# Attention scores on one core: the first key load as two halves of 128 partitions, or as four loads of every fourth partition

## The chip, the cores and the metric

The kernel runs on one NeuronCore of a Trainium2 chip. The metric is device time in microseconds (us) for one execution. The engines are TensorE (PE, with its weight loads shown as PEld), VectorE (DVE), ScalarE (ACT), GpSimd (POOL) and SyncE (SP). Loads and stores run on the core's 16 DMA engines. SyncE and ScalarE issue them here, each in a queue of its own.

## The reference

```python
def setup_inputs():
    batch, heads, seq, dim = 8, 8, 512, 64
    return {"q": randn(batch, heads, seq, dim), "k": randn(batch, heads, seq, dim)}   # float32

def reference(q, k):
    scale = 1.0 / np.sqrt(q.shape[-1])
    return (np.einsum('bhqd,bhkd->bhqk', q, k) * scale).astype(np.float32)
```

For each of 64 pairs of batch and head, a 512 x 64 matrix q is multiplied with the transpose of a 512 x 64 matrix k. The inputs have 8.4 MB each, the output has 67.1 MB.

## The kernel before, in words

**Units and loads.** The batches are taken two at a time: four units (`UNITS`), each with 2 MB of k and 2 MB of q. A load (`load`, L68) brings one of these into one half of a buffer `big` in the on-chip memory: 128 partitions with one row of 16 KB each. The partition number is made of the index (s h m), which runs over half of the heads and over blocks of 64 sequence rows, and of (b x), which is the batch of the unit and the half of the heads. (b x) has four values and is the fast part: partition = 4 x (s h m) + (b x). In DRAM the 32 rows of one value of (b x) lie one behind the other, 512 KB in all, and the four values lie 512 KB apart.

**The first k load** is cut in two halves of the rows (L74 to L78): each half goes to all 128 partitions with 8 KB a row. SyncE issues the first half, ScalarE the second, both ahead of the program's opening barrier (L80). Each half has its own semaphore (`halves`).

**SyncE's order** is written out by hand. After the barrier it issues the next five loads (L91: q of unit 0, then k and q of units 1 and 2). It then waits twice for casts, because unit 3 shares a buffer with unit 1, and issues k and q of unit 3 (L93 to L95). Then come sixteen stores of 4 MB (L96 to L99), each behind a wait for the results of its group, and at last a wait for all stores (L102).

**GpSimd** (L105 to L122) turns each load into bf16 and writes it in another order into `xb`: two casts for each load, one for each half of the rows. For the first k load the first cast waits for the first half alone and the second cast for the second half. Each load that has been cast counts up `ready`.

**VectorE** transposes blocks of 32 x 32 out of `xb` into `kT` (L148, keys) and `qz` (L156, queries), and shares with ScalarE the work of taking results out of PSUM: ScalarE multiplies by the scale at L186 (80 tiles), VectorE at L189 (48 tiles). **TensorE** does 256 matmuls (L140).

**Buffers.** Three buffers `big` of 4 MB serve the loads and then the stores in turn (`store_buffer`, L62). TensorE does not start a group before the store that used its buffer three groups earlier has landed, nor, for the first groups, before the loads in that buffer have been cast.

Of the kernel before, what the change touches and what calls it, by code (L numbers as in the profile page):

```python
# [5 lines left out]
def kernel(  # L6
# [5 lines left out]
    nc = tc.nc  # L12
    B, H, S, D = q.shape
    scale = 1.0 / (D ** 0.5)
    P = 128
# [4 lines left out]
    R = S // M  # L20
# [12 lines left out]
    names = ["ready", "zeroed", "pe", "act", "dve"]  # L33
    sem = {name: nc.alloc_semaphore(name) for name in names}
    load_sems = [nc.alloc_semaphore(f"load{n}") for n in range(2 * UNITS)]
    halves = [load_sems[0], nc.alloc_semaphore("load0b")]
    store_sems = [nc.alloc_semaphore(f"store{n}") for n in range(3)]


# [18 lines left out]
    def xf(v):  # L58
        return bigs[(0, 1, 2, 1)[v]].rearrange("p x i k -> p (x i k)").rearrange(
            "p (x s c) -> p x s c", x=2, s=2)  # L60
# [4 lines left out]
    def rows(v, x):  # L65
        return (k_r, q_r)[x][v]

    def load(v, x):  # L68
        nc.sync.dma_start(out=xf(v)[:, x].rearrange("p s c -> p (s c)"), in_=rows(v, x)
                          ).then_inc(load_sems[2 * v + x], 16)  # L70

    for s, queue in enumerate((nc.sync, nc.scalar)):  # L74
        first_load = queue.dma_start(
            out=xf(0)[:, 0, s], in_=rows(0, 0)[..., s * R * D // 2:(s + 1) * R * D // 2]
        ).then_inc(halves[s], 16)
        tc.no_tile_sem_insts.add(first_load.ins.name)  # L78
    tc.close()
    tc.compile()  # L80

# [6 lines left out]
        return who, g * takers.count(who) + takers[:p + 1].count(who)  # L88


    for n in range(1, 2 * (UNITS - 1)):  # L91
        load(n // 2, n % 2)
    for x in range(2):  # L93
# [10 lines left out]

    for v in range(UNITS):  # L105
        for x in range(2):
            if v or x:
                nc.gpsimd.wait_ge(load_sems[2 * v + x], 16)
            for s in range(2):
                if v == x == 0:  # L110
                    nc.gpsimd.wait_ge(halves[s], 16)
                src = xf(v)[:, x, s]
                dst = xb[:, 2 * v + x]
                if x == 0:
                    src = src.rearrange("p (w e d) -> p w e d", e=2, d=D)
                    dst = dst[:, s * J // 2:(s + 1) * J // 2].rearrange("p w d e -> p w e d")
                else:
                    src = src.rearrange("p (jj e i d) -> p jj e i d", e=2, i=RO, d=D)
                    dst = dst.rearrange("p (i jj) d e -> p jj e i d", i=RO)[
                        :, s * JJ // 2:(s + 1) * JJ // 2]  # L120
                cast = nc.gpsimd.tensor_copy(out=dst, in_=src)  # L121
            cast.then_inc(sem["ready"], 1)  # L122
# [3 lines left out]
    for pair in range(ALL * PAIRS):  # L126
        g, p = divmod(pair, PAIRS)
        n, i = g % 4 * 2 + p // 4, p % 4 * 2
# [51 lines left out]
    for pair in range(ALL * PAIRS):  # L180
        g, p = divmod(pair, PAIRS)
# [43 lines left out]
```

## Time and profile before

| What | us |
|---|---|
| Median of 6 runs (201.37 to 201.61) | 201.49 |
| The profiled execution | 201.37 |
| Its span, from the first to the last instruction | 200.1 |
| PE busy | 85.4 |
| DVE busy | 154.9 |
| ACT busy | 79.4 |
| POOL busy | 38.9 |
| First half of k, from issue to landing (SyncE) | 5.9 |
| Second half of k, from issue to landing (ScalarE) | 10.5 |
| Stores, from issue to landing, median (longest) | 15.1 (22.8) |

The span begins at the first instruction; all times in views of the profile count from there. A line of the profile's page or of the timeline names the engine, the line of the kernel (L121 is line 121), the operation, what is written and what is read (`xb<-big`) and the shapes. "SPq" and "ACTq" are the issues of transfers by SyncE and ScalarE. An issue is not the transfer: the bytes move afterwards, and the landing is when the last of them is in place. The waits of an engine are listed as: engine and line, what it waited for, microseconds in total, how often, longest.

### The profile page before, as it was taken

How to read it: one execution, taken by the hardware profiler on the slowest of the kernel's cores; microseconds unless marked ns; L12 is line 12 of the kernel's file. 1: busy time of each engine (PE TensorE's matmuls, PEld its weight loads, DVE VectorE, ACT ScalarE, POOL GpSimd, SP SyncE). 2: the span in 40 equal slices, each digit the busy share in tenths (PEclk: the TensorE clock that was granted, in tenths of full speed). 3: DMA queues.
4: the chain of work that ended last, by engine and by line, in shares of the span. 5: the costliest groups of instructions: out<-in, count | busy, mean ns of one | idle time of the engine just before them, and what ended most of it. 6: DMA issues, size and time to landing. Idle time of an engine off the chain costs nothing.

```text
span 200.1 us, 784 instructions
## 1 busy us (share of the span) xinstructions
PE 85.4 (43%) x251; PEld 27.3 (14%) x256; DVE 154.9 (77%) x97; ACT 79.4 (40%) x81; POOL 38.9 (19%) x20
## 2 busy tenths in 40 slices
PE   0000064474932474547355825572374557910000
PEld 0000021121311121112111211121121112200000
DVE  2428959996999899989998999999989996830000
ACT  2000026272763285248423942583347344940000
POOL 0479999986000000000000000000000000000000
PEclk9999999666698597558755896879759555995555
DMA  5999999999999999999999999999999999999996
GB/s 187 442 419 449 426 423 432 419 367 439 439 432 419 432 436 442 414 426 432 449 419 424 436 442 426 419 429 446 436 419 429 436 436 423 423 432 449 426 419 288
DMA packets 5652, 83.94 MB, mean 420 GB/s; under 512 B 400, under 2 KB 400, under 8 KB 400
## 3 DMA queue, kind: packets, MB, share of 16 engines
q1 hardware_dynamic: 5504, 82.84, 97.5%
q10 hardware_dynamic: 144, 1.05, 1.2%
q8 instruction: 2, 0.03, 0.1%
q14 instruction: 2, 0.02, 0.0%
HBM read 16.78 MB, written 67.11 MB: 419 GB/s over the span
## 4 chain that ended last, share of the span: by engine, by line
DVE 54%; DMA 13%; POOL 11%; PE 6%; ACT 4%; issue 1%
DVE qz L156 24%; DVE big L189 18%; DVE kT L148 12%; POOL xb L121 11%; DMA big<-in_q_dram 8%; PE ps L140 6%; DMA big<-in_k_dram 5%; ACT big L186 4%
## 5 line engine op out<-in xcount | busy, mean ns | idle before, releaser
L140 PE MATMUL ps<-kT,qz 128*128 128x512 bf16 x251 | 85.4, 495 | 90.7 <-DVE big L189 57.2
L186 ACT ACTIVATE big<-ps 128x1024 f32<-128x1024 f32 x80 | 78.1, 1028 | 95.2 <-PE ps L140 92.5
L189 DVE TENSOR_SCALAR big<-ps 128x1024 f32<-128x1024 f32 x48 | 57.7, 1218 | 9.7 <-PE ps L140 9.4
L156 DVE STREAM_TRANSPOSE qz<-xb 32x1024 f32<-32x1024 f32 x32 | 64.1, 2003 | 1.2 <-POOL xb L121 0.7
L140 PEld LDWEIGHTS ps<-kT,qz 128*128 128x128 bf16 x256 | 27.3, 119 | 148.3 <-DVE big L189 76.0
L121 POOL CAST xb<-big 128x2048 bf16<-128x2048 f32 x16 | 38.7, 2474 | 9.1 <-DMA big<-in_k_dram 8.4
L148 DVE STREAM_TRANSPOSE kT<-xb 64x1024 f32<-64x1024 f32 x16 | 31.2, 1947 | 7.3 <-POOL xb L121 6.9
L171 DVE MEMSET qz<- 128x4096 uint32 x1 | 3.5, 3472 | 3.5 <-PEq L80 3.5
L186 ACT ACT_TABLE_LOAD x1 | 1.3, 1283 | 2.6 <-PEq L80 2.6
L209 POOL MEMSET const-float32-0.0<- 128x1 f32 x1 | 0.1, 98 | 0.2 <-issue 0.2
L209 POOL MEMSET const-bfloat16-1.0<- 128x1 bf16 x1 | 0.1, 101 | 0.0
L209 POOL MEMSET const-uint8-127<- 128x1 uint8 x1 | 0.1, 101 | 0.0
L209 POOL MEMSET const-float32-1.0<- 128x1 f32 x1 | 0.1, 98 | 0.0
## 6 DMA issues: line engine op xcount, KB each, us to landing
out_dram<-big SPq DMA_DIRECT2D x16, 4096.0 KB, 15.1
big<-in_q_dram SPq DMA_DIRECT2D x4, 2048.0 KB, 17.3
big<-in_k_dram SPq DMA_DIRECT2D x3, 2048.0 KB, 15.1
big<-in_k_dram SPq DMA_DIRECT2D x1, 1024.0 KB, 5.9
big<-in_k_dram ACTq DMA_DIRECT2D x1, 1024.0 KB, 10.5
```

The lines of the kernel that those rows point to most:

```text
L121: cast = nc.gpsimd.tensor_copy(out=dst, in_=src)
L140: ins = pe.matmul(out=pss[pair % 4][:, w, :], lhsT=qz[:, n, i + w], rhs=kT[:, n], start=True, stop=True)
L148: return nc.vector.transpose(out=kw[2 * y * Q:2 * (y + 1) * Q, b % 2 * G:(b % 2 + 1) * G].rearrange("d g (m w) -> d w m g", w=J), in_=xw[s ...
L156: return nc.vector.transpose(out=qw[d:d + Q, b % 2 * G:(b % 2 + 1) * G, :, h * Q:(h + 1) * Q].rearrange("d g i (m jj) -> d i jj m g", jj=J ...
L171: nc.vector.memset(qz, 0.0).then_inc(sem["zeroed"], 1)
L186: nc.scalar.mul(out=o, in_=ps, mul=scale).then_inc(sem["act"], 1)
L189: nc.vector.tensor_scalar(out=o, in0=ps, scalar1=scale, scalar2=None, op0=mult).then_inc(sem["dve"], 1)
L209: nc = _bacc.Bacc("TRN2", target_bir_lowering=False, num_devices=1)
```

## The change

The first k load becomes four loads instead of two. Load n takes one value n of (b x): 512 KB that lie in one run in DRAM, to the 32 partitions n, n + 4, n + 8 and so on, with a full row of 16 KB each. SyncE issues load 0 and ScalarE load 1 ahead of the barrier. SyncE issues loads 2 and 3 after the barrier, ahead of the five loads that stood there. Each load has its own semaphore, and GpSimd waits for all four before its first cast; the two casts themselves stay as they were.

```diff
-    halves = [load_sems[0], nc.alloc_semaphore("load0b")]
+    parts = [load_sems[0]] + [nc.alloc_semaphore(f"load0_{n}") for n in range(1, 4)]
...
-    for s, queue in enumerate((nc.sync, nc.scalar)):
-        first_load = queue.dma_start(
-            out=xf(0)[:, 0, s], in_=rows(0, 0)[..., s * R * D // 2:(s + 1) * R * D // 2]
-        ).then_inc(halves[s], 16)
-        tc.no_tile_sem_insts.add(first_load.ins.name)
+
+    def load_part(queue, n):
+        dst = xf(0)[:, 0].rearrange("p s c -> p (s c)")[n:P:4]
+        return queue.dma_start(out=dst, in_=rows(0, 0)[:, n]).then_inc(parts[n], 16)
+
+    for n, queue in enumerate((nc.sync, nc.scalar)):
+        tc.no_tile_sem_insts.add(load_part(queue, n).ins.name)
     tc.close()
     tc.compile()
...
+    for n in (2, 3):
+        load_part(nc.sync, n)
     for n in range(1, 2 * (UNITS - 1)):
         load(n // 2, n % 2)
...
     for v in range(UNITS):
         for x in range(2):
-            if v or x:
-                nc.gpsimd.wait_ge(load_sems[2 * v + x], 16)
+            for part in [load_sems[2 * v + x]] if v or x else parts:
+                nc.gpsimd.wait_ge(part, 16)
             for s in range(2):
-                if v == x == 0:
-                    nc.gpsimd.wait_ge(halves[s], 16)
                 src = xf(v)[:, x, s]
                 dst = xb[:, 2 * v + x]
```

## The prediction

> **What bounds the kernel now.** I read the profile in this order: the page's busy rows and DMA row, the busy time by stage, SyncE's own waits, the timeline of the first microseconds, the chain of waits, and last the trace's packet and landing records, of which the page prints only the sums.
>
> The page first. The digits are tenths of each of 40 slices; the queue line gives packets, MB and the share of 16 DMA engines' time.
>
> ```profile
> span 200.1 us, 784 instructions
> ...
> DMA  5999999999999999999999999999999999999996
> ...
> q1 hardware_dynamic: 5504, 82.84, 97.5%
> ...
> HBM read 16.78 MB, written 67.11 MB: 419 GB/s over the span
> ```
>
> VectorE, the busiest compute engine, has 77%; the DMA engines have 9 in every slice but the first and the last. The busy time by stage says the same (columns: window, length, busy time and count of PE, PEld, DVE, ACT, POOL, PE clock, DMA share, GB/s):
>
> ```profile
> 0.00:2.10 2.10, 0.00 (x0) 0.00 (x0) 0.00 (x0) 0.00 (x0) 0.20 (x4) 1.00 0.00 0
> 2.10:5.00 2.90, 0.00 (x0) 0.00 (x0) 1.46 (x1) 1.28 (x1) 0.00 (x0) 1.00 1.01 322
> 5.00:13.50 8.50, 0.00 (x0) 0.00 (x0) 2.01 (x1) 0.00 (x0) 4.62 (x2) 1.00 1.03 438
> ...
> 40.00:42.20 2.20, 2.20 (x6) 0.71 (x5) 2.15 (x3) 1.88 (x2) 2.20 (x2) 0.50 1.13 343
> 42.20:177.30 135.10, 75.58 (x225) 24.02 (x228) 125.99 (x82) 70.42 (x73) 5.46 (x3) 0.74 1.01 430
> 177.30:198.20 20.90, 0.00 (x0) 0.00 (x0) 0.00 (x0) 0.00 (x0) 0.00 (x0) 0.56 1.00 427
> ```
>
> For the last 21 us no engine computes at all while the DMA still moves 427 GB/s. SyncE's waits agree:
>
> ```profile
> SPq L98 <- DVE big L189: 141.3, 16, 11.3
> SPq L102 <- DMA out_dram<-big: 22.4, 2, 19.3
> ```
>
> It waits 22.4 us for stores to land after it has issued the last one at 177.3. So when the last result is ready, over two stores of 4 MB are still queued, and compute could be some 10 us later at no cost. The page's chain of waits gives VectorE 54%, but it runs through work that the queue covers: the end is set by how many bytes the DMA engines have to move and by when they are held up.
>
> This can be added up. By the packet records each engine moves 312 rows of 16 KB (median 0.611 us) and 16 rows of 8 KB (0.309 us): 190.6 + 4.9 = 195.6 us. Add 2.15 us before the first byte, some 0.35 us of slow first rows, 0.5 us lost at 40 to 42 us (343 GB/s where 430 is usual), and some 1.3 us by which instruction fetches at 80 to 108 and 159 us put one engine behind: 199.9. The last landing is at 200.0. Nothing that shortens compute is in this sum.
>
> **The change part by part.** *What the compute engines gain is hidden.* Timeline (start, duration, what):
>
> ```profile
> 0.73 0.63 SPq L75 DMA_DIRECT2D big<-in_k_dram  x1
> 0.74 0.66 ACTq L75 DMA_DIRECT2D big<-in_k_dram  x1
> 2.61 0.54 SPq L69 DMA_DIRECT2D big<-in_q_dram  x1
> ...
> 6.72 2.45 POOL L121 CAST xb<-big 128x2048 bf16<-128x2048 f32 x1 [6.28 <-DMA big<-in_k_dram]
> 11.33 31.47 POOL L121 CAST xb<-big 128x2048 bf16<-128x2048 f32 x13 [2.16 <-DMA big<-in_k_dram]
> 13.89 3.97 DVE L148 STREAM_TRANSPOSE kT<-xb 64x1024 f32<-64x1024 f32 x2 [6.87 <-POOL xb L121]
> ```
>
> Today the second half of k lands at 11.28 because ScalarE's rows take turns with the first q load. After the change all four parts stand ahead of q, so at the usual pace k would be complete near 2.15 + 0.35 + 8 x 0.611 + 0.1 = 7.5 us. But POOL now waits for all four before its first cast: casts at 7.5 and 10.0, end 12.4, and VectorE starts 1.4 us earlier than at 13.89. That lead dies at once: q lands at 13.42 today (issue 2.61, 10.8 us to landing) and the bytes ahead of it stay the same, so POOL, which starts q's casts at 13.8, gains at most 0.4 us there. After that a load of 2 MB lands every 4.89 us and POOL's two casts take 4.84, so POOL follows the landings. I cost this part at nothing. What hides it is the queue of stores; without that cover it would be worth at most 0.4 us. The two further waits on POOL hold back only casts of the same k; VectorE's first transpose is behind them, covered as above.
>
> *SyncE's queue.* Two issues more stand at 2.6 and 3.2 us, each 0.53 to 0.63 us by the load rows, so the five loads behind them leave SyncE 1.2 to 1.3 us later: the first q load at 3.85 instead of 2.61. By the first load, bytes start 1.42 us after the issue starts (0.73 to 2.15). So part 3 would start by 4.0 us, part 4 by 4.7, q by 5.3. Parts 1 and 2 give each engine four 16-KB rows, which keep it busy to 2.15 + 0.35 + 4 x 0.611 = 4.95. The margin is 0.9 us; q has more. Cost nothing; without the margin see the rivals. No later load or store moves past another.
>
> *The rows.* Per engine 16 rows of 0.309 us go and 8 rows of 0.611 come: -0.06 us. Two more loads mean two more completion writes on each engine, 9 ns each: +0.02.
>
> *The issue itself.* The stores' issues take 0.372 us, the loads' 0.53 to 0.66. If a load with one plain run of DRAM is issued like a store, the first byte comes 0.26 us earlier. Bounds -0.26 to 0; I take 0, the load rows being nearest.
>
> *How fast the 32-partition loads run.* This is the open cost, and everything hangs on it. Every load and store of this trace covers 128 partitions, eight rows on each engine for a load, and ran at 0.611 us a row with no row of two engines in each other's way. None covers 32 partitions, four apart; how two rows per engine are dealt, and whether engines then get in each other's way, no row shows. Low end: 0.611 us a row, cost 0. High end: engines slow each other to half the pace, 8 x 0.611 = +4.9 us. Between them stands the only place where all engines ran slow, where the last load meets the first store:
>
> ```profile
> 41.00:42.00 1.00, 1.00 (x4) 0.34 (x3) 0.97 (x2) 1.00 (x2) 1.00 (x1) 0.50 0.79 229
> ```
>
> There 39 rows took 0.65 to 1.18 us, mean 0.91. I take that mean for the eight rows: 8 x (0.91 - 0.61) = +2.4 us. I choose the middle row and not the low end because the new loads change exactly what kept the rows even: the one pattern of 128 partitions in which all 16 engines keep step.
>
> [...]
>
> The sum: -0.06 + 0.02 + 0 + 2.4 = +2.4 us. Since the DMA engines have no idle time later, what is lost at the start is still lost at the end. The profiled execution took 201.37 us (its span 200.1 and 1.3 around it), 0.12 below the median of 201.49: 203.8 on it, 203.9 on the median.
>
> **The rivals.**
>
> *The parts run at full pace and nothing else counts.* For it: the same bytes, rows of 16 KB as in every other load, and a gain in compute that is hidden. Against it: only that no such load is in the trace. Sum -0.04: 201.4, within 0.2% (0.4 us, about what a measurement of this kernel can tell from no change).
>
> *A shorter start: faster.* The place is 0.7 to 3.5 us. The issue may shorten by 0.26 us; and four engines took 1.27 to 1.38 us over their first row where the others took 0.97, and stay 0.45 us behind. If reading one plain run evens that out, up to 0.26 + 0.45 + 0.04 = 0.75 us goes, less if another engine is last. It decides once rows run at 0.611 us and more than 0.4 us of the start goes: 200.7 to 201.1, say 200.9. Against it: the first row of any engine has to wait for its first bytes.
>
> *The DMA runs dry* between parts 2 and 3. For it: only 1 MB is queued before SyncE passes the barrier at 2.6 us, where 2 MB was. The first q load's first row came 4.0 us after its issue; if that were its own delay and not the queue ahead of it, part 3 would come at 6.6, 1.67 us after the engines ran out: 203.1. Against it: every engine took its first ScalarE row after exactly seven SyncE rows, the slow engines 0.4 us later than the rest; so that wait counts rows ahead, not time.
>
> *The chain of waits is right* and POOL's earlier start reaches the end: 0.4 us at q, 1.4 at most, so 200.1 to 201.1. Against it: the 22.4 us of queued stores.
>
> **How the numbers follow.** Slowed rows 0.50 (its own range 201.7 to 206.3, from almost none of the cost to all of it; 0.04 of the chance lies under 201.9); full pace 0.26; shorter start 0.14; dry 0.05, nearly all of it slower; chain 0.05. Faster by over 0.2%: 0.14 + 0.04 of the chain = 0.18. Slower: 0.46 + 0.04 = 0.50. Within: 0.26 + 0.04 + 0.02 = 0.32. The likeliest case gives 203.9. The range for 8 in 10 leaves out about 0.1 at the top, the slowed rows nearest to half pace, and 0.1 at the bottom: 200.9 to 205.8.
>
> **What would show it.** Right: k's rows longer than 0.611 us between 2.2 and 10 us; some 300 GB/s from 2 to 12 us, where 403 stands today; q's landing near 15.8 instead of 13.4; every later landing as much later; the rate after 42 us unchanged. Full pace: k complete near 7.5, q still at 13.4. Dry: a gap in the DMA row near 5 us. Shorter start: first byte before 2.1 us, and the whole series of landings earlier by as much. The prediction is wrong above all if eight rows of k take 0.611 us each; then only the start is left to move the end.

## The result, and the profile after

The changed kernel took 201.92 us (median of 20 runs, 201.29 to 202.77) against 201.54 us (median of 40 runs, 201.34 to 201.79) in the same sessions: ratio 1.0022, 95% interval 1.0014 to 1.0029. So it is slower by 0.4 us, where 2.4 us was forecast. Its runs are spread over 1.5 us, those of the kernel before over 0.45. The profiled execution took 202.13 us, with a span of 200.8, 0.76 longer than the span before; it stands in the upper half of the runs, and the profiled execution of the kernel before (201.37) in the lower half of its own. So the two profiles differ by twice the difference of the medians.

The page after, the same rows as before:

```profile
span 200.8 us, 788 instructions
...
DMA  6999999999999999999999999999999999999996
...
q1 hardware_dynamic: 5504, 83.36, 97.9%
q10 hardware_dynamic: 48, 0.52, 0.7%
...
HBM read 16.78 MB, written 67.11 MB: 418 GB/s over the span
```

Little has changed here: ScalarE's queue (q10) carries one load of 0.5 MB where it had one of 1 MB, and SyncE's (q1) carries those 0.5 MB more. The difference shows only by stage (columns as above: the GB/s stand last):

```profile
2.10:5.00 2.90, 0.00 (x0) 0.00 (x0) 1.52 (x1) 1.28 (x1) 0.00 (x0) 1.00 1.03 379
5.00:13.50 8.50, 0.00 (x0) 0.00 (x0) 1.95 (x1) 0.00 (x0) 4.60 (x2) 1.00 0.99 380
...
40.00:42.20 2.20, 2.20 (x7) 0.76 (x5) 2.19 (x2) 1.46 (x2) 2.20 (x2) 0.50 1.07 432
42.20:177.30 135.10, 77.03 (x228) 24.42 (x231) 126.88 (x83) 70.87 (x74) 6.92 (x3) 0.75 1.01 429
177.30:198.20 20.90, 0.00 (x0) 0.00 (x0) 0.38 (x1) 1.00 (x2) 0.00 (x0) 0.60 1.01 428
```

Three things are to be seen. The first 3 us are faster than before (379 against 322 GB/s). The next 8.5 us are slower (380 against 438): 58 x 8.5 = 0.49 MB is missing, 1.1 us at 430 GB/s. And at 40 to 42 us, where the kernel before fell to 343, this one keeps 432. SyncE's waits are as before:

```profile
SPq L102 <- DVE big L191: 140.8, 16, 11.3
SPq L106 <- DMA out_dram<-big: 22.1, 2, 19.3
```

The timeline of the start (start, duration, what):

```profile
0.73 2.94 SPq L77 DMA_DIRECT2D big<-in_k_dram  x3
0.74 0.57 ACTq L77 DMA_DIRECT2D big<-in_k_dram  x1
...
3.73 1.67 SPq L69 DMA_DIRECT2D big<-in_q_dram  x1
...
8.90 4.81 POOL L123 CAST xb<-big 128x2048 bf16<-128x2048 f32 x2 [8.46 <-DMA big<-in_k_dram]
13.82 3.91 DVE L150 STREAM_TRANSPOSE kT<-xb 64x1024 f32<-64x1024 f32 x2 [6.87 <-POOL xb L123]
```

k is complete at 8.75 us, not at 7.5, so VectorE starts at 13.82 and has won 0.07 us instead of 1.4. The issue of the first q load, at 3.73 as forecast, holds SyncE for 1.67 us where it took 0.54 before.

**The account of the last engine.** A load or store has landed when the last of the 16 DMA engines has finished its share. The trace records when each of them has; here are the mean and the last of the 16, in us:

| Landing | before, mean / last | after, mean / last | last: after minus before |
|---|---|---|---|
| first q load | 13.14 / 13.42 | 13.76 / 14.90 | +1.48 |
| load before the last (k of unit 3), before the turn | 37.61 / 37.88 | 38.23 / 39.35 | +1.47 |
| last load (q of unit 3), after the turn at 40 us | 43.10 / 43.28 | 43.18 / 44.34 | +1.06 |
| third store | 72.30 / 72.46 | 72.32 / 73.56 | +1.10 |
| fourth store, after an instruction fetch at 81 us | 82.18 / 83.40 | 82.12 / 83.27 | -0.13 |
| fifth store | 91.89 / 93.07 | 91.90 / 93.17 | +0.10 |
| twelfth store | 160.01 / 160.99 | 160.25 / 161.10 | +0.11 |
| thirteenth store, after an instruction fetch at 160 us | 169.81 / 171.00 | 170.13 / 171.74 | +0.75 |
| last store | 198.99 / 200.03 | 199.51 / 200.79 | +0.76 |

This is the account of the two profiles. The start costs 0.62 us on the mean of the engines and 1.48 on the last. The turn from loads to stores gives 0.54 of the mean back and 0.41 of the last. At 80 to 82 us instructions are fetched: the packet records have one packet of 8 KB and one of 16 KB, each in the place of a row, so that sixteen packets run at any time as before. In the change the two overlap (81.40 to 81.71 and 81.68 to 82.64 us), so there they go through two engines. In the kernel before, the larger one took 1.01 us, the row that starts where it ends took 1.01 instead of 0.61, and at the next landing one engine is 1.2 us behind the mean. Before, this is the new last engine; after, another is that late already, and the last landing moves no further. At 160 us another fetch of 16 KB costs the last engine 0.6 us more after than before. That the fetches are the cause is read from the times alone.

**Where the start is lost.** The trace does not name the engine of a packet, but in the first microseconds nearly every row starts within a few nanoseconds of the end of another, so the rows can be put in order for each of the 16 engines. What the rows of the changed kernel take beyond 0.611 us each:

| Rows | First row, median / longest | Beyond 0.611 us each, sum per engine |
|---|---|---|
| part 1 of k (SyncE, ahead of the barrier) | 0.87 / 1.12 | 0.31 |
| part 2 (ScalarE, ahead of the barrier) | 0.61 / 1.03 | 0.08 |
| part 3 (SyncE, after the barrier) | 0.82 / 1.51 | 0.32 |
| part 4 (SyncE, after the barrier) | 0.63 / 0.84 | 0.11 |
| q | 1.06 / 2.10 | 0.54 |

The eight rows of k so lose 0.82 us on each engine. In the kernel before, the eight rows of 8 KB of the first half lose 0.79 (beyond 0.309 us each) and those of the second half nothing, so k costs no more than before. What is new is q: 0.54 us in its rows, above all in the first one, and 0.10 us in which engines had no row between 6 and 7 us. With the first byte 0.07 us earlier, this makes 0.82 - 0.79 + 0.54 + 0.10 - 0.07 = 0.60 of the 0.62 us. In the second profile of the change q's first row takes 0.98 us (longest 1.51); with all four parts ahead of the barrier (below) it takes 0.61 (longest 0.74).

### The profile page after: what moved, and what is told of

The parts are those of the page before. It is cut to its first block, busy times and chain, and to the rows that moved or that the text cites. A ratio compares the mean times of both kernels' runs of the same rounds, so it can differ in the third digit from the quotient of the medians.

```text
span 200.8 us, 788 instructions
## 1 busy us (share of the span) xinstructions
PE 85.6 (43%) x251; PEld 27.4 (14%) x256; DVE 154.9 (77%) x97; ACT 79.4 (40%) x81; POOL 39.0 (19%) x20
## 4 chain that ended last, share of the span: by engine, by line
DVE 54%; DMA 17%; PE 7%; POOL 5%; ACT 3%; SPq 2%; issue 1%
DVE qz L158 24%; DVE big L191 18%; DMA big<-in_q_dram 17%; DVE kT L150 12%; PE ps L142 7%; POOL xb L123 5%; ACT big L188 3%; SPq L69 1%; SPq L77 1%
```

## The experiments

Theory A was the prediction's: rows to 32 partitions four apart run slowly. Theory B: small loads ahead of q leave the engines a short queue. Theory B2: each further load costs by itself. Theory C: the turn at 40 us takes back what the start wins or loses. Theory D: what is lost at the start is lost at the end. Theory E: the end goes with the engine that is last. "On the mean" and "on the last" are the mean and the last of a load's 16 landings. Ratios are against the kernel before in the same session, with their 95% interval.

**The change once more.**

> The changed kernel once more, for a second profile of the same program. In its first profile the first q load landed between 13.24 and 14.90 us over the 16 DMA engines (before: 12.95 to 13.42), the rows of 2.1 to 10 us were long, the 40 to 42 us stall of the kernel before was missing, and the last store ended 0.76 us later. Theory A (loads into 32 partitions four apart run unevenly): latest landing of q again 14.5 to 15.2, ratio 1.002. Theory B (what counts is that the first loads are small and SyncE issues q late): the same here; the next runs tell them apart. Theory C (the difference is a matter of chance in where engines stand): another spread, latest landing anywhere from 13.4 to 15.

Measured: ratio 1.0033 (1.0021 to 1.0045). q at 13.67 on the mean, 14.65 on the last engine. The start is much the same as in the first profile, and so is the account against the first profile of the kernel before: +1.23 on the last engine at q, +0.76 at the last load, -0.41 at the fourth store, +1.05 at the end. So theory C as stated here (chance in the start) falls; the loss at the start is the change's.

**Quarter rows to all partitions.**

```diff
-        dst = xf(0)[:, 0].rearrange("p s c -> p (s c)")[n:P:4]
-        return queue.dma_start(out=dst, in_=rows(0, 0)[:, n]).then_inc(parts[n], 16)
+        cut = slice(n * R * D // 4, (n + 1) * R * D // 4)
+        dst = xf(0)[:, 0].rearrange("p s c -> p (s c)")[:, cut]
+        return queue.dma_start(out=dst, in_=rows(0, 0)[..., cut]).then_inc(parts[n], 16)
```

> Four loads of 512 KB in the same queues, at the same places and with the same waits as in the change, but each takes a quarter (4 KB) of the row of all 128 partitions. Theory A (32 partitions four apart): back to the kernel before: q's latest landing near 13.4, spread over the engines 0.5, ratio 0.999 to 1.001. Theory B (small loads, late q): like the change, q's latest landing near 14.9, ratio 1.002 or more.

Measured: ratio 1.0055 (1.0041 to 1.0070), q at 13.86 on the mean and 15.10 on the last. So 128 partitions do not take the loss away. But its place is another one: the windows show the loss ahead of 5 us, where the rows of 4 KB start slowly, and not behind it.

```profile
2.00:5.00 3.00, 0.00 (x0) 0.00 (x0) 1.47 (x1) 1.28 (x1) 0.00 (x0) 1.00 0.88 246
5.00:10.00 5.00, 0.00 (x0) 0.00 (x0) 2.01 (x1) 0.00 (x0) 0.00 (x0) 1.00 1.07 423
```

The changed kernel in the same windows:

```profile
2.00:5.00 3.00, 0.00 (x0) 0.00 (x0) 1.52 (x1) 1.28 (x1) 0.00 (x0) 1.00 1.04 377
5.00:10.00 5.00, 0.00 (x0) 0.00 (x0) 1.95 (x1) 0.00 (x0) 1.10 (x1) 1.00 1.00 351
```

So this run does not tell A from B.

**All four parts ahead of the barrier.**

```diff
-    for n, queue in enumerate((nc.sync, nc.scalar)):
+    for n, queue in enumerate((nc.sync, nc.scalar, nc.sync, nc.scalar)):
...
-    for n in (2, 3):
-        load_part(nc.sync, n)
```

> The change, but all four loads are issued ahead of the barrier, two by SyncE and two by ScalarE, so that neither k nor q comes late to an idle engine. Theory A: rows of k as long as in the change, q's latest landing 14.5 to 15, ratio about 1.002. Theory B: no dry engine, q's latest landing 13.3 to 13.6, ratio 0.999 to 1.000.

Measured: ratio 1.0011 (1.0002 to 1.0021). q at 12.75 on the mean and 13.13 on the last, better than the kernel before by 0.39 and 0.29. From 2.8 to 7.5 us the rows have a median of 0.611 us. The windows:

```profile
2.00:5.00 3.00, 0.00 (x0) 0.00 (x0) 0.88 (x1) 1.28 (x1) 0.00 (x0) 1.00 0.99 410
5.00:10.00 5.00, 0.00 (x0) 0.00 (x0) 2.59 (x1) 0.00 (x0) 1.53 (x1) 1.00 0.99 416
```

The same four loads to the same partitions now run at full pace from the start: theory A falls, and B2 with it. The start is 0.4 us shorter than before, and yet the kernel is not faster: at 40 to 42 us the engines lose more (below). The profile is of the fastest of the eleven runs (201.40; median 201.74).

**Both loads of the first unit in parts.** The list of parts grows to eight, four for k and four for q; SyncE issues six of them after the barrier, and GpSimd waits for the four of a load before its casts.

```diff
-        dst = xf(0)[:, 0].rearrange("p s c -> p (s c)")[n:P:4]
-        return queue.dma_start(out=dst, in_=rows(0, 0)[:, n]).then_inc(parts[n], 16)
+        dst = xf(0)[:, n // 4].rearrange("p s c -> p (s c)")[n % 4:P:4]
+        return queue.dma_start(out=dst, in_=rows(0, n // 4)[:, n % 4]).then_inc(parts[n], 16)
...
-    for n in (2, 3):
-        load_part(nc.sync, n)
-    for n in range(1, 2 * (UNITS - 1)):
+    for n in range(2, 8):
+        load_part(nc.sync, n)
+    for n in range(2, 2 * (UNITS - 1)):
```

> The suspected cost doubled: both k and q of the first unit come in four loads of every fourth partition, SyncE issuing six of them after the barrier. Theory A: the next k load (18.32 at the latest in the kernel before, 19.76 in the change) lands 1.2 us later on the mean of the engines than in the kernel before, twice the 0.62 of the change, and up to 3 us later on the last one: 19.8 to 21.3; ratio 1.004 to 1.010. Theory B: 19.3 to 20.0, as in the change, ratio 1.002 to 1.004.

Measured: ratio 1.0035 (1.0020 to 1.0049). The next k load lands at 18.30 on the mean and 18.67 on the last: 0.27 and 0.35 behind the kernel before, less than half of what the change loses there. Twice the parts are half the loss; neither A nor B2 nor my number for B foresaw that. The profile is of one of the faster runs (201.67, where the median is 202.11), so the loss in the others may be larger.

**The second half of k after the barrier**, in the kernel before:

```diff
-    for s, queue in enumerate((nc.sync, nc.scalar)):
-        first_load = queue.dma_start(
-            out=xf(0)[:, 0, s], in_=rows(0, 0)[..., s * R * D // 2:(s + 1) * R * D // 2]
-        ).then_inc(halves[s], 16)
-        tc.no_tile_sem_insts.add(first_load.ins.name)
+    def load_half(s):
+        return nc.sync.dma_start(
+            out=xf(0)[:, 0, s], in_=rows(0, 0)[..., s * R * D // 2:(s + 1) * R * D // 2]
+        ).then_inc(halves[s], 16)
+
+    tc.no_tile_sem_insts.add(load_half(0).ins.name)
...
+    load_half(1)
     for n in range(1, 2 * (UNITS - 1)):
```

> The kernel before with one edit: the second half of k is issued by SyncE after the barrier, ahead of q, so that only 1 MB is queued until then, as in the change. Loads still go to 128 partitions in rows of 8 KB. Theory B (a short queue at the start: loads that come to engines with little left to do run slowly and unevenly): the rows of 5 to 10 us get longer, q lands 0.4 to 0.8 us later than before on the mean of the engines (13.14) and 1 us or more on the last one (13.42): 14.2 to 15; ratio 1.001 to 1.005. Theory B2 (each further load costs by itself, however long the queue): as before, q at 13.0 to 13.5, ratio 0.999 to 1.001.

Measured: ratio 1.0011 (0.9996 to 1.0026): no difference is shown. But the twelve runs fall in two groups: nine from 201.38 to 201.71 us and three from 202.52 to 203.01, where the longest of the kernel before beside them is 201.81. The profile (202.76) is of one of the three. In it q lands at 13.06 on the mean and 13.88 on the last: q's mean is not late, only a few engines are, and the last landing of all comes 1.36 us later than in the first profile of the kernel before (201.39 against 200.03). That agrees with theory E; the other nine have no profile. So with 1 MB queued and one load of 1 MB ahead of q, the mean loses nothing. A short queue alone is not enough: theory B can hold only with q issued as late as in the change (3.73 and held to 5.40; here 2.98 to 3.57).

**Two loads of every second partition, ahead of the barrier.**

```diff
-        dst = xf(0)[:, 0].rearrange("p s c -> p (s c)")[n:P:4]
-        return queue.dma_start(out=dst, in_=rows(0, 0)[:, n]).then_inc(parts[n], 16)
+        dst = xf(0)[:, 0].rearrange("p s c -> p (s c)")[n:P:2]
+        return queue.dma_start(out=dst, in_=rows(0, 0)[:, n:4:2]).then_inc(parts[n], 16)
...
-    for n in (2, 3):
-        load_part(nc.sync, n)
```

The list of parts has two entries here.

> Two loads of 1 MB, both ahead of the barrier, one by SyncE and one by ScalarE, each to every second partition with rows of 16 KB; POOL waits for both. Theory B: the queue is as long as before, rows of 16 KB start faster than rows of 8 KB, as when all four parts stood ahead of the barrier: q lands near 12.75 on the mean, 13.2 at the latest. Theory B2: two loads, so as before: 13.1. Theory A (partitions apart run unevenly), which the last runs spoke against: 14 or more. For the end, theory C (the turn from loads to stores at 40 us gives back what the start wins or loses, and the end goes with the last engine): ratio 0.999 to 1.001, although the start is 0.4 us shorter; without theory C 0.998.

Measured: ratio 1.0010 (1.0002 to 1.0019). q at 12.86 on the mean and 13.21 on the last, the last load at 43.23 on the mean (before: 43.10): 0.28 us won at the start, gone at the turn.

**Parts 2 and 3 by ScalarE.**

```diff
     for n in (2, 3):
-        load_part(nc.sync, n)
+        load_part(nc.scalar, n)
```

> The change, but loads 2 and 3 are issued after the barrier by ScalarE, so that SyncE issues q at once, at 2.6 us. Theory B: the queues are deep early, rows between 5 and 10 us have the usual length, the next k load lands at 17.5 to 18.2 instead of 18.65 (mean); ratio 1.000 to 1.001. Theory B2: still four loads, 18.6; ratio 1.002.

Measured: the next k load at 17.69 on the mean and 18.08 on the last, 0.34 and 0.24 ahead of the kernel before. With q issued at 2.54 us the loss at the start is gone, with the same loads and partitions. Yet the ratio is 1.0035 (1.0023 to 1.0047). k is complete only at 10.8 us, so POOL's first cast starts at 10.92 us, and the first store is issued at 38.3 us instead of 36.4; the turn loses 1.1 us on the mean, where the kernel before loses 0.6. That the late k is what this pays for was not tested by itself.

**One whole load by SyncE ahead of the barrier**, nothing by ScalarE: `dst` is the whole of `xf(0)[:, 0]`, the source `rows(0, 0)`.

> One load of 2 MB by SyncE ahead of the barrier, 128 partitions, rows of 16 KB, nothing by ScalarE. Theory B and theory B2 alike: a long queue and one load: q lands at 12.6 to 12.9 on the mean. Theory C: all the same the end stays, ratio 0.999 to 1.001; without theory C 0.998 or less.

Measured: q at 12.87 on the mean; ratio 1.0017 (1.0008 to 1.0025). Again a start won and an end not.

**Both halves after the barrier**, in the kernel before:

```diff
-    for s, queue in enumerate((nc.sync, nc.scalar)):
-        first_load = queue.dma_start(
...
+    for s, queue in enumerate((nc.sync, nc.scalar)):
+        queue.dma_start(
+            out=xf(0)[:, 0, s], in_=rows(0, 0)[..., s * R * D // 2:(s + 1) * R * D // 2]
+        ).then_inc(halves[s], 16)
     for n in range(1, 2 * (UNITS - 1)):
```

> The kernel before with both halves of the first k load issued after the barrier instead of ahead of it, so that all engines start some 1.9 us later and in step. In the runs so far the last load landed at 43.0 to 43.5 us on the mean of the engines, whether the load before it had landed at 37.3 or at 38.3. Theory D (time lost at the start is lost at the end, as the prediction had it): last load at 45.0, ratio 1.009 to 1.010. Theory C (the turn from loads to stores gives the difference back, up to the 0.5 us or so that engines stand there): last load at 44.3 to 44.6, ratio 1.005 to 1.008.

Measured: the halves are issued at 1.38 us, not at 2.6, because without them the barrier itself is over sooner; the first byte moves at 2.79 instead of 2.15. So the start is 0.64 us late, not 1.9, and my numbers have to be scaled. The last load lands at 43.86 on the mean, 0.76 late; ratio 1.0033 (1.0021 to 1.0046), 0.67 us. Here engines that were late in step lost about as much at the end, as theory D has it, and theory C's "the turn gives it back" falls as a rule. That 0.64 and 0.67 agree so well is in part luck: q is only 0.47 us late on the mean, and the turn then adds 0.3.

**One engine late**, in the kernel before: one small load more after the barrier, 17 rows of 2 KB to 17 partitions. `extra` is a buffer of its own that nothing reads; SyncE waits for `extra_sem` at the end. The 1.0 to 1.5 us below take all 17 rows to be one engine's, which was my assumption: at the pace of 16 KB in 0.611 us they are an estimated 1.3 us for it and 0.08 us on the mean of the 16.

```diff
...
+    nc.sync.dma_start(out=extra[0:17], in_=k.rearrange("b h (r e) d -> (b h r) (e d)", e=8)[0:34:2]
+                      ).then_inc(extra_sem, 16)
     for n in range(1, 2 * (UNITS - 1)):
```

> [...] Theory E (the end goes with the engine that is last, so a single late engine is enough): one landing of every load 1.0 to 1.5 us after the others, end 0.1 to 1.3 us later, ratio 1.001 to 1.006, and a spread over the runs as wide as that of the change. Theory D (bytes over the mean rate): ratio 1.000 to 1.001.

Measured: ratio 1.0096 (1.0081 to 1.0110), 1.8 us for 34 KB. q lands at 13.25 on the mean (before 13.14) and at 14.69 on the last (13.42): 0.11 and 1.27 us later, which fits the assumption; no record names the engine of a row. (The further issue also makes SyncE issue q 0.36 us later, at 2.97.) Theory E holds, at a higher price than I gave it. Not only does the last engine end later; at 70 to 72 us engines run out of work:

```profile
70.00:72.00 2.00, 1.91 (x7) 0.63 (x8) 2.00 (x2) 1.02 (x1) 0.00 (x0) 0.77 0.83 352
```

TensorE starts a group when a store three groups earlier has landed on the last engine; the results of that group are the store for which the first engine waits. With the landings 3.0 us apart, the fourth store is issued 0.7 us before the first engine has finished the third; the first load took 1.42 us from issue to first byte (0.73 to 2.15 in the kernel before). 0.3 us on the mean of the engines is idle there. The rest comes in small portions: from 45 to 198 us a row takes 0.617 us on the mean, where it takes 0.612 in the kernel before, and the last store lands 1.46 us later on the mean and 1.61 on the last.

**The first store by ScalarE**, in the kernel before (`for g in range(1, ALL)` for SyncE), and **the same with all four parts ahead of the barrier**:

```diff
+        if pair == PAIRS - 1:
+            for who in ("act", "dve"):
+                nc.scalar.wait_ge(sem[who], takers.count(who))
+            nc.scalar.dma_start(out=out_r[0, 0, 0], in_=store_buffer(0).rearrange("p x i k -> p x (i k)")
+                                ).then_inc(store_sems[0], 16)
```

> The kernel before, but the first store is issued by ScalarE in its own queue, so that its rows take turns with the last load's rows instead of following them. If the stand at 40 to 42 us comes from all engines turning from loads to stores one behind the other, it goes: rows near 0.611 us from 38 to 46, ratio 0.997 to 0.998. If it comes from loads and stores that run at the same time, it gets longer: ratio 1.001 to 1.005.

> All four parts ahead of the barrier (q landed 0.4 us earlier there, and the turn took it back) together with the first store by ScalarE. If the turn is eased by this, both gains stay: ratio 0.995 to 0.997. If not: 1.000 to 1.005.

Measured: ratios 1.0119 (1.0104 to 1.0133) and 1.0101 (1.0085 to 1.0116). The last load now shares the engines with the store and lands at 45.7 instead of 43.1 us, the groups that need its buffer start later, and the dip comes earlier (279 GB/s from 39 to 40 us in the first) instead of going away. Up to the third store the first of the two is not behind for all that: it lands at 72.02 on the mean and 72.28 on the last (before: 72.30 and 72.46). But its fourth store is issued only 0.46 us before the first engine has finished the third, and from 70 to 74 us the engines have no row for 0.7 us on the mean. No version here beats the kernel before.

**The kernel before once more.**

> The kernel before once more, for a second profile. Theory E needs the last engine's account to be the same: q's latest landing 13.3 to 13.6, the latest landing of the stores 1.1 to 1.3 us further behind at the first instruction fetch (80 us) and 0.2 to 0.4 at the second (160 us). If these differ by more than 0.5 us between two profiles of one kernel, the account explains single executions and not the median.

Measured: q's last landing at 13.15 (expected 13.3 or more); the spread of the landings grows from 0.6 to 2.0 us at the first fetch, and the last landing is 0.2 us further behind than in the first profile at the second; end 200.33 against 200.03. The account is the same within 0.3 us. At 39.5 to 42.5 us it has the same dip:

```profile
39.50:42.50 3.00, 3.00 (x9) 1.07 (x8) 2.96 (x3) 1.94 (x2) 3.00 (x2) 0.51 0.92 300
```

The first profile of it has 306 there; the change:

```profile
39.50:42.50 3.00, 3.00 (x8) 1.07 (x9) 2.99 (x2) 1.76 (x2) 3.00 (x2) 0.50 0.97 399
```

and all four parts ahead of the barrier:

```profile
39.50:42.50 3.00, 3.00 (x12) 1.15 (x10) 2.96 (x3) 2.38 (x3) 3.00 (x2) 0.72 0.93 268
```

**q ahead of parts 2 and 3**, in the change:

```diff
+    load(0, 1)
     for n in (2, 3):
         load_part(nc.sync, n)
-    for n in range(1, 2 * (UNITS - 1)):
+    for n in range(2, 2 * (UNITS - 1)):
```

> The change with one edit: SyncE issues the first q load right after the barrier and loads 2 and 3 of k behind it. Theory B (the loss at the start is that of a short queue while SyncE issues small loads ahead of q): q's issue at 2.6 us, no held issue, the next k load lands at 17.6 to 17.9 on the mean and 18.0 to 18.4 at the latest (change: 18.65 and 19.76); ratio 1.000 to 1.002. Theory B2 (each small load costs): 18.5 or more, ratio 1.002 or more.

Measured: the next k load at 17.75 on the mean and 18.10 on the last: q issued at 2.54 takes the loss at the start away, as with ScalarE. But the ratio is 1.0145 (1.0128 to 1.0162), far outside. k is complete only at 13.2 us:

```profile
13.30 38.19 POOL L124 CAST xb<-big 128x2048 bf16<-128x2048 f32 x16 [12.85 <-DMA big<-in_k_dram]
```

POOL then casts without a pause and is behind the loads all the way; VectorE starts at 18.22 us instead of 13.89. The first results come late, and the second store is issued 0.6 us after the first one has begun to land:

```profile
50.00:52.00 2.00, 0.71 (x4) 0.31 (x4) 2.00 (x2) 0.03 (x1) 1.49 (x1) 1.00 0.64 270
52.00:54.00 2.00, 2.00 (x6) 0.59 (x5) 1.83 (x3) 1.50 (x2) 0.00 (x0) 0.53 0.46 197
```

The engines stand idle for 1.8 us on the mean. My theories priced the transfers alone and forgot who waits for k.

**Neighbouring partitions**, with all four parts ahead of the barrier; part of the keys then stands in other partitions than the transposes assume, so the output is not the reference's.

```diff
-        dst = xf(0)[:, 0].rearrange("p s c -> p (s c)")[n:P:4]
+        dst = xf(0)[:, 0].rearrange("p s c -> p (s c)")[n * 32:(n + 1) * 32]
```

> All four parts ahead of the barrier, but each goes to 32 neighbouring partitions instead of every fourth one; the keys of the first unit then stand in other partitions than the transposes assume, so part of the output is not the reference's. By the prediction's idea that the dealing of rows decides, this or the version with every fourth partition has rows of about 1.2 us: k complete near 12, q near 17.5. If dealing costs nothing either way: rows of 0.61 to 0.63 as there, q at 12.7 to 12.9 on the mean.

Measured (one run): 205.15 us, 201.43 for the kernel before beside it. q at 17.46 on the mean, and rows of 1.24 us (mean of the first load's rows after the start), twice 0.611:

```profile
2.00:5.00 3.00, 0.00 (x0) 0.00 (x0) 1.69 (x1) 1.28 (x1) 0.00 (x0) 1.00 0.92 202
5.00:10.00 5.00, 0.00 (x0) 0.00 (x0) 1.78 (x1) 0.00 (x0) 0.00 (x0) 1.00 1.00 210
```

So rows went down to half the pace here, as the prediction's high end had it, but with 32 neighbouring partitions and not with every fourth. What slows them is not shown.

## Why the prediction was right or wrong

Slower was forecast and slower it is, but by another step than the one that carried the forecast, and by a sixth of its size; the sign came out right by luck. The step that failed is the term of +2.4 us for slowed rows of the 32-partition loads: k's rows lose no more than in the kernel before (0.82 against 0.79 us on each engine). In its place the runs show a loss where the prediction put nothing, in SyncE's queue: q, issued behind two small loads, starts slowly on engines that have little queued, 0.62 us on the mean and 1.48 on the last engine.

**The end is set by the bytes: right, with a wrong margin.** The DMA has work until the end in all versions. But "compute could be some 10 us later at no cost" is true of the last stores alone, from which I read it. The trace has the row that I should have taken: in the kernel before, a store is issued 4.6 us before the first engine has finished the store ahead of it in the early groups, but only 2.0 us before at the tightest, and if a store needs as long to its first byte as the first load, 1.42 us of that are gone. So I estimate the cover at 0.6 us in that profile, and at none in the second profile of the same kernel, whose tightest lead is 1.28 us. In the change the tightest lead is 1.35 us, and rows grow on the mean from 0.611 us at 45 to 80 us to 0.616 in the last third of the run; in the two profiles of the kernel before they reach 0.612 and 0.614 there. So short leads and long rows go together, but the tightest lead alone does not order the cases. When VectorE's first transpose came 4.3 us later than in the kernel before (q ahead of parts 2 and 3), 2.9 us came out at the end.

**POOL's earlier start is hidden: right in its effect.** The reason given was not put to the test, since k was complete 1.3 us later than worked out and there was hardly a gain to hide (0.07 us at VectorE).

**SyncE's queue, "cost nothing": wrong, by omission.** The issues took 0.49 and 0.58 us, as worked out, and q's issue began at 3.73 instead of 3.85. But q's issue then held SyncE to 5.40, and the rows of 7 to 9 us took 0.79 us on the mean. I asked only whether an engine would run dry; it hardly does (0.1 us on the mean at 6 to 7 us). What costs is the first row of a load that comes late: 0.82 us for part 3 and 1.06 for q in the median, up to 2.10 on one engine, where a row behind others takes 0.611. This is +0.62 us on the mean at q's landing and +1.48 on the last engine. With q issued at 2.54, or all parts ahead of the barrier, it is gone. That the engines had too few rows queued is the reading that fits these runs; that q's issue was held, and for how long, goes with it in both profiles of the change and was not separated from it. The rival "dry" came nearest, but its sign, a gap, did not show and its price (1.67) was too high.

**The rows and the issue: right in size.** The first byte moves at 2.08 instead of 2.15 us, an issue takes 0.57 us instead of 0.63; rows of 16 KB start faster than rows of 8 KB (410 GB/s from 2 to 5 us with all parts early, against 311 and 339 in the two profiles of the kernel before), more than the 0.06 us given. One reading of the prediction is off: of the first rows, four took 1.27 to 1.38 us, but the other twelve took 0.70 to 0.97, not 0.97 alike. The rival "a shorter start" was there too, at 0.4 us, in the versions that issue everything early.

**Slowed rows, +2.4 us: wrong, and the step that failed.** In every fourth partition the rows take their 0.611 us (median with all parts ahead of the barrier). I took a price from the one place where all engines ran slow, a turn from loads to stores, though it had nothing in common with the change but slowness. Half pace, the prediction's high end, came with 32 neighbouring partitions: rows of 1.24 us and 210 GB/s from 5 to 10 us, where every fourth partition, issued as early, had 416.

**"What is lost at the start is still lost at the end": half right.** Late in step, 0.64 us became 0.67 (both halves after the barrier). But 0.4 us won by all engines was given back at the turn, and 34 KB of further load (by my estimate 0.08 us on the mean), which made q's last landing 1.27 us later, cost 1.8. The end goes more with the last engine than with the mean at the start.

**What stays open.** At the turn the engines lose between 0.0 and 1.1 us on the mean (the time between the landings of the last two loads, less 4.89 us): 0.6 and 0.7 in the kernel before, 0.1 and 0.0 in the change, 0.9 with all parts early, but 0.9 also with both halves after the barrier, where everything comes late, and 1.0 in the profile with the second half late, where the landings are 1.0 us apart. So neither the time nor the spread of the landings orders the cases, and the cause is open. Nor is it shown which of the late engines an instruction fetch hits, nor what held SyncE for 1.67 us. Of the three versions that take the loss at the start away, one comes nearer to the kernel before (1.0011, where the change has 1.0022 and 1.0033), the others do not (1.0035 and 1.0145). So the loss at the start is shown to be the change's, and the account above follows it to the end in two profiles of each kernel; that it makes 0.4 us in the median is not derived.

## What to carry to other kernels

When a kernel is bound by its transfers, follow the last landing of each load and store from the start to the end and not the mean rate: a last landing that came 1.3 us later at q (14.69 against 13.42) cost 1.8 us here, while 0.4 us won on the mean of all engines came to nothing. Ask of a load that is split not only whether the queue runs dry but what is issued behind it and how much later: the pieces cost next to nothing (ratio 1.0011) when all of them and the next load were queued early. And measure the cover of a compute chain at its tightest store, not at the last one.

## What the runs showed of the hardware that was not expected

- A load of 2 MB in four pieces to 32 partitions each, all issued ahead of the barrier, ran at the pace of the other loads (median 0.611 us for a row of 16 KB) with partitions four apart, and at half of it (mean 1.24 us, one run) with neighbours.
- Instruction fetches of 8 and 16 KB took the place of rows on the DMA engines. In the kernel before, the 16 KB at 80.9 us took 1.01 us and the row behind it 1.01 instead of 0.61; one landing was then 1.2 us behind the mean, and one was still 1.0 behind at the end.
- A load started slowly on engines that hardly ran dry: the first rows of part 3 and of q took 0.82 and 1.06 us in the median (up to 2.10) in the change, where a row usually takes 0.611, while 13 of the 16 engines had gaps of less than 0.1 us in all from the first row on.
- With one load of 17 rows of 2 KB ahead of q, q's last landing was 1.4 us behind the mean (14.69 against 13.25), where it was 0.3 (13.42 against 13.14).
- With both halves of k taken from ahead of the barrier, the barrier ended sooner: the first half, issued behind it, was issued at 1.38 us, 0.65 us later than before and not 1.9.
